# Ordering the products that use a part of the TensorE array, with four key tiles and two weight staging tiles, in a decoder layer with sparse attention

## The chip, the core and the metric

The kernel runs on one core of a Trainium2 chip. TensorE (PE) multiplies: it holds a stationary operand in its array of 128 x 128 cells, streams a moving operand through it and writes PSUM. VectorE (DVE), ScalarE (ACT) and GpSimd (POOL) compute; SyncE (SP) issues most loads, POOL issues the gathers by index. The metric is the device time of one execution in microseconds (us), lower is better. Products of 128 x 32 cells use one of four column groups of the array, products of 128 x 64 one of two, and products over 64 rows one of two row groups; products on different groups can be in the array at the same time.

## What is computed

One inference step of a decoder layer for a prompt of 512 tokens and for 8 samples of 4 new tokens each, whose 4096 past keys and values lie in pages of a cache. Model width 1024, hidden width of the feed-forward 2816. Cut to what matters here:

```python
x = x + 0.5 * swiglu(rmsnorm(x), ffn1)
h = rmsnorm(x)
gb, gc, hc, q, k, v, qi, ki, wi = split(h @ w_in)     # 3 x 512, 512, 128, 128, 512, 64, 8 columns
y_conv = gb * short_conv(gc * hc)                     # depthwise, width 3
I[t, s] = sum_h wi[t, h] * relu(qi[t, h] . ki[s])     # indexer, 8 heads of 64
idx = top_k(I masked causally)                        # 128 of the prompt's, 256 of a sample's 4100 keys
attn = softmax(q . k[idx] / 8) @ v[idx]               # 8 query heads of 64 on 2 key heads
x = x + concat(y_conv, attn) @ w_out
x = x + 0.5 * swiglu(rmsnorm(x), ffn2)
```

All is fp32. The selected keys aren't gathered one by one: all logits are made, and those not selected get a bias of -1e30.

## The kernel before, in words

The activations lie transposed on the chip, 544 tokens (32 of the samples, 512 of the prompt) in columns. The weights of the feed-forward layers, of w_in and of w_out are streamed (`stream`, L155): a staging tile wst of 128 x 1024 fp32 (tag "wst", WB of them) is loaded by SP, ACT rounds it to a high part whi, DVE or POOL subtracts that to get a low part wlo, and PE then makes three products (high by high, high by low, low by high) in fp32r at one pass each. whi and wlo have three places ("slots"). wst is free again when wlo is made, except in `nat` for the 32 sample tokens (i = 0, L522), which multiplies by the fp32 tile itself, a quarter of the products in each column group. `load_half` (L588) loads the columns of one group of w_in in runs of k-tiles: two tiles for most groups, three (KS) for the second half of the indexer's columns, which comes first.

Between the feed-forward layers lies the mixer (L1307). Its parts are Python generators, each a row of steps, and `plan` (L1255) emits the steps in order of a start and a spacing for each part (PLAN for the first half, PLAN2 for the second). The framework then orders the instructions of each engine by priority and by when their operands and buffers are expected to be there; LAG shifts the priority of a part, and parts in PINNED keep the program's order on PE. What an engine issues is fixed when the program is built. The parts: A, B indexer columns; Q, K queries, keys and values; S the samples' indexer scores; V the exact search of each sample query's 256th best score (DVE, three searches of two bits a round), which ends with `self.bias` (L870); I, D the prompt's scores and selection (DVE); L the raw logits of the first four samples; e, c the gated convolution in four chunks, with three tiles of w_in columns each (e, the chunks 0 and 1, uses slot 2 only); then s the attention of the samples, P that of the prompt, w the first half of w_out.

The products that the change touches:

- S, `sample_scores` (L709): for each of 8 steps (a half of the pages and a pair of samples) two gathers of index keys by POOL, each transposed by PE in `key_transpose` (L699, eight transposes to PSUM "KTp", copied by ACT to one of KTB tiles "KT"); `scores` (L743) then multiplies them for the pair, 64 columns of the array each, two halves of 512 keys (ssc); `gathered` (L754) sums heads for four pairs, 32 columns each (SC).
- L and s, `qk` (L1023): logits of one quarter of the pages for four samples. For each sample a gather of keys and a key_transpose; two products of 32 columns and 512 keys each (lg) follow, LGD = 2 samples behind. Each sample writes its own 32 partitions of one PSUM tile with tag "w".
- s, `pv` (L1094): the values of a quarter: four gathers, eight transposes of the weights (PT), 32 products of 32 columns (O), four samples for each of eight key tiles.
- `sample_attend` (L1121): after the softmax of samples 0 to 3, four times pv of these and qk of samples 4 to 7, then the softmax and four pv of these. Keys and values share KV = 4 gather tiles.
- P, `prompt_softmax` (L1156): for a block of 128 queries four logits products over 64 rows of the array (plg), each into its own PSUM tile with tag "f", and read by DVE.

PSUM has tags w (two tiles of two banks; used by KTp, lg, ssc, PT and the feed-forward's G, U, Y), f (two of one bank), s and t (one each). `mm` (L129) issues a product; `keep_in_program_order` pins it.

Of the kernel before, what the change touches and what calls it, by code (L numbers as in the profile page):

```python
# [15 lines left out]
ALU = mybir.AluOpType  # L16
# [30 lines left out]
WB = 3  # L47
# [9 lines left out]
LGD = 2  # L57
KTB = 3
# [59 lines left out]
class Trunk:  # L118
# [14 lines left out]
    def tp(self, *args):  # L133
        ins = self.nc.tensor.transpose(*args)  # L134
        return self.tc.keep_in_program_order(ins) if self.pin else ins

# [18 lines left out]
    def stream(self, srcs, n, m, kind="", slot=None):  # L155
        """fp32 weights [128, n, m] from DRAM, as the two float32r parts, in the given or the next place of three."""
# [25 lines left out]
    def wmm(self, unit, parts, act, cuts=HALVES, which=(0, 1)):  # L182
        """unit[:, i, :] = W^T act over all k-tiles, for the ith cut of the tokens; W stationary."""
# [10 lines left out]
    def fmm(self, name, parts, act, n):  # L194
        """two PSUM banks, one per half of the tokens: W^T act over n k-tiles."""
# [35 lines left out]
    def rms(self, ssq):  # L231
        """sums of squares [128 tokens, 5 tiles] -> rn, 1 / root mean square."""
# [19 lines left out]
    def spread(self):  # L252
        """R [128, T]: the row of rn on every partition."""
# [9 lines left out]
    def ffn(self, wg, wu, wd, done, late=False):  # L263
# [3 lines left out]
        def hidden(f, G, U):  # L267
            """G, U: one PSUM tile of equal halves, or (columns, PSUM) pairs."""
# [95 lines left out]
    def begin_units(self):  # L364
        """loads and transposes the activations; the first gate and up units, by halves of the tokens as these come in."""
        nc, tc, i = self.nc, self.tc, self.i
        with tc.tile_pool(name="init", bufs=1) as ip, tc.high_priority(offset=FIRST):
# [13 lines left out]
            def weights(w, n):  # L381
                """w's first 128 columns in n runs of k-tiles: for each a function that loads it, fp32 and the two parts."""
# [57 lines left out]
            def mms(unit, w, hf, order="01234567" * 2):  # L440
                """the high parts of the weights at a k-tile's first mention, the low ones at its second."""
# [80 lines left out]
    def nat(self, i, wparts, m):  # L522
        """steps; PSUM [tokens of tile i, m]. The few samples take a column group of the array each for a quarter of the
        fp32 products, and the four sums are added at the end."""
# [29 lines left out]
    def rope(self, v, i, n, nh, kind):  # L554
        """partial rotary on v [n tokens, nh, 64] of token tile i."""
# [32 lines left out]
    def load_half(self, pieces, m, ks=(4, 4), slots=(0, 1)):  # L588
        """w_in columns in runs of ks k-tiles, [128, k, m] each; pieces: (offset in tile, first column, width)."""
# [8 lines left out]
    def later(self, f, depth):  # L598
        """keep f for later; run what lies deeper than depth."""
        if f:  # L600
            self.held.append(f)
        while len(self.held) > depth:
            self.held.pop(0)()

    def idx_group(self, g, i, parts, depth=0):
        """steps; four indexer query heads of token tile i, and for g = 1 the indexer keys and head weights."""
# [45 lines left out]
    def qkv_group(self, g, i, parts, depth=0):  # L652
        """steps; four query heads of token tile i (g: 0, 1), or its keys and values (g: 2)."""
# [45 lines left out]
    def key_transpose(self, kn, name):  # L699
        """eight 128 x 128 transposes of gathered keys, PSUM -> SBUF."""  # L700
# [8 lines left out]
    def sample_scores(self, mp):  # L709
        """indexer scores of the sample queries over all pages: [128 = (bp, jh, b2, rr, t), (jl, p)]."""  # L710
# [20 lines left out]
        def headsum(out, S, bp, jh):  # L731
            self.mm(out, wm[:, bp, jh, :], S, start=True, stop=True)
# [10 lines left out]
        def scores(n):  # L743
            bp = n % 4
            w = self.wunit("ssc")
            for hf in range(2):
                for b2 in range(2):
                    self.mm(w[64 * b2:64 * b2 + 64, hf, :], self.qbi[:, 2 * bp + b2].rearrange("p r t h -> p (r t h)"),
                            kts[n, b2][:, hf * 512:(hf + 1) * 512], start=True, stop=True)
# [4 lines left out]
        def gathered(jh, c):  # L754
            u = self.tunit("SC")
            for bp in range(4):
                headsum(u[32 * bp:32 * bp + 32, :], SS[bp][:, c * 512:(c + 1) * 512], bp, jh)
# [43 lines left out]
    def sample_select(self, mp):  # L801
        """exact top K_S of the 4100 scores of each query (ties: lowest position first) -> bias 0 / -BIG."""
# [16 lines left out]
        def search(src, bits, base0):  # L819
            """[128, 1]: the largest x of base0 to base0 + 2**bits - 1 with K_S elements of the query at or above x,  # L820
            two bits a round: three candidates, counted on the vector engine (two) and the scalar engine."""
# [82 lines left out]
    def prompt_scores(self, pool):  # L904
        """indexer scores of prompt blocks 1..3, causally filled; block 0 keeps every admissible key."""
# [27 lines left out]
    def prompt_select(self, pool, scores):  # L933
        """the top K_P of the scores of each query (ties: lowest position first) -> 0 / -BIG."""
# [13 lines left out]
    def conv(self, cs, pool, early=False):  # L948
        """steps; the gated convolution of the channel chunks cs."""
# [73 lines left out]
    def qk(self, st, q, more):  # L1023
        """PSUM: raw logits of quarter q of the pages, samples 4 st to 4 st + 3; rows (b, g, c, t)."""
        nc = self.nc
        kts, w = [], None

        def logits(b4):
            for rr in range(2):
                self.mm(w[32 * b4:32 * b4 + 32, rr, :], self.qbd[:, 4 * st + b4].rearrange("p g c t -> p (g c t)"),  # L1030
                        kts[b4][:, rr], start=True, stop=not more)

        for b4 in range(4):
# [3 lines left out]
            if b4 >= LGD:  # L1037
                w = w or self.wunit("lg")
                logits(b4 - LGD)
        for b4 in range(4 - LGD, 4):  # L1040
            yield
            w = w or self.wunit("lg")
            logits(b4)
# [195 lines left out]
    def until(self, mark, steps):  # L1239
        """advance steps until mark is reached."""  # L1240
        while mark not in self.done:
            next(steps)
# [273 lines left out]
```

## Time and profile before

| | |
|---|---|
| three runs | 1279.54, 1279.09, 1273.50 us, median 1279.09 |
| profiled execution, span from first to last instruction | 1270.2 us; its device time is not in the profile |
| PE busy | 1230.0 us, 97% |
| DVE, ACT, POOL busy | 640.4, 456.4, 209.3 us |
| stages | feed-forward 1 to about 411 us, mixer to about 860 us, feed-forward 2 |
| mean granted TensorE clock | 0.995 of full |

The span runs from the first to the last instruction of the core; the device time of a run has some more around it. Busy times are unions: an fp32 product shows as two matmul records, a record's duration runs to its modelled end, and records that overlap count once. A group of products that run one behind the other and one that run together can so have the same mean duration; the union and the starts tell them apart.

### The profile page before, as it was taken

What the parts mean: (1) busy time and instruction counts of PE and PEld (TensorE: products, weight loads), DVE (VectorE), ACT (ScalarE), POOL (GpSimd) and SP (SyncE); (2) the same over time, 40 slices, a digit from 0 to 9 for tenths busy, and PEclk for the clock granted to TensorE, in tenths of its full rate; (3) what the DMA queues carried; (4) which work ended last, traced back from release to release, by engine and by line L of the source; (5) the groups of instructions that cost most, each with busy time, mean ns of one, the idle gap of its engine ahead of it and who ended that gap; (6) DMA issues with size and microseconds to landing.
All of it is one profiled execution on the core that took longest, in us unless ns stands there. A gap on an engine that the chain in (4) does not pass through costs nothing.

```text
span 1270.2 us, 22873 instructions
## 1 busy us (share of the span) xinstructions
PE 1230.0 (97%) x9629; PEld 1112.8 (88%) x9629; DVE 640.4 (50%) x1230; ACT 456.4 (36%) x696; POOL 209.3 (16%) x319
## 2 busy tenths in 40 slices
PE   9999999999999999899989989999999999999998
PEld 8999999999999747776667545789999999999998
DVE  5444334433446216999999753265443344433442
ACT  6332122212224464456525556244222122222222
POOL 3200000000000646665413231310000000000000
PEclk9999999999999999999999999999999999999999
DMA  7422332332222553245224443543223323322322
GB/s 231 133 85 84 93 90 84 92 92 84 86 73 69 179 178 106 68 138 169 68 61 140 161 151 124 167 141 113 87 84 93 91 84 87 96 85 84 91 75 74
DMA packets 184363, 136.10 MB, mean 107 GB/s; under 512 B 5706, under 2 KB 172434, under 8 KB 184260
## 3 DMA queue, kind: packets, MB, share of 16 engines
q1 hardware_dynamic: 171700, 91.62, 24.7%
q0 software_dynamic: 11904, 42.26, 10.3%
q8 instruction: 76, 1.25, 0.4%
q10 hardware_dynamic: 656, 0.76, 0.2%
q14 instruction: 27, 0.22, 0.1%
HBM read 131.66 MB, written 2.96 MB: 106 GB/s over the span
## 4 chain that ended last, share of the span: by engine, by line
PE 83%; DVE 10%; DMA 2%; issue 2%; ACT 1%; POOL 1%; DVEq 0%; ACTq 0%; POOLq 0%
PE Y L191 20%; PE U L191 20%; PE G L191 19%; PE Yo L130 4%; DVE flip L829 3%; PE KTp L134 2%; PE lg L130 2%; PE nat L130 2%; DMA ckn<-in_cache_k,ik 2%; PE O L130 2%; PE ssc L130 1%; PE plg L130 1%; PE pO L130 1%; DVE pw L928 1%; PE gc L130 1%
## 5 line engine op out<-in xcount | busy, mean ns | idle before, releaser
L166 ACT ACTIVATE whi<-wst 128x1024 fp32r<-128x1024 f32 (+3 forms) x173 | 172.7, 999 | 582.6 <-PE Y L191 181.2
L171 DVE TENSOR_TENSOR wlo<-wst,whi 128x1024 fp32r<-128x1024 f32 (+3 forms) x156 | 180.7, 1158 | 26.8 <-ACT whi L166 23.1
L191 PE MATMUL Y<-hh,wlo 128*128 128x272 f32 (+2 forms) x704 | 147.6, 288 | 0.0
L191 PE MATMUL Y<-hh,whi 128*128 128x272 f32 (+2 forms) x704 | 147.4, 289 | 0.0
L191 PE MATMUL Y<-hl,whi 128*128 128x272 f32 (+2 forms) x704 | 147.1, 288 | 0.0
L191 PE MATMUL U<-xh,whi 128*128 128x272 f32 x688 | 142.0, 287 | 1.5 <-DVE t L274 1.5
L191 PE MATMUL U<-xh,wlo 128*128 128x272 f32 x688 | 141.6, 288 | 0.0
L191 PE MATMUL U<-xl,whi 128*128 128x272 f32 x688 | 141.3, 287 | 0.0
L191 PE MATMUL G<-xh,whi 128*128 128x272 f32 x656 | 135.6, 287 | 0.0
L191 PE MATMUL G<-xl,whi 128*128 128x272 f32 x656 | 135.0, 287 | 0.0
L191 PE MATMUL G<-xh,wlo 128*128 128x272 f32 x656 | 134.9, 288 | 0.0
L276 DVE TENSOR_TENSOR u<-U,R 128x544 f32<-128x544 f32 x43 | 31.2, 725 | 160.2 <-PE U L191 160.2
L191 PEld LDWEIGHTS Y<-hl,whi 128*128 128x128 f32 x704 | 111.4, 188 | 0.0
L191 PEld LDWEIGHTS Y<-hh,whi 128*128 128x128 f32 x704 | 111.1, 188 | 0.0
L191 PEld LDWEIGHTS Y<-hh,wlo 128*128 128x128 f32 x704 | 110.7, 189 | 0.0
L330 DVE SCALAR_TENSOR_TENSOR x<-Y,x 128x544 f32<-128x544 f32 x46 | 33.3, 725 | 152.2 <-PE Y L191 152.2
L191 PEld LDWEIGHTS U<-xh,whi 128*128 128x128 f32 x688 | 107.1, 188 | 1.6 <-ACT whi L166 1.6
L191 PEld LDWEIGHTS U<-xl,whi 128*128 128x128 f32 x688 | 107.5, 188 | 0.0
L191 PEld LDWEIGHTS U<-xh,wlo 128*128 128x128 f32 x688 | 107.1, 189 | 0.0
L169 POOL TENSOR_TENSOR wlo<-wst,whi 128x1024 fp32r<-128x1024 f32 (+2 forms) x17 | 34.4, 2025 | 423.4 <-ACT whi L166 422.8
L191 PEld LDWEIGHTS G<-xl,whi 128*128 128x128 f32 x656 | 102.6, 188 | 0.0
L191 PEld LDWEIGHTS G<-xh,whi 128*128 128x128 f32 x656 | 102.2, 188 | 0.0
(330 smaller groups left out, 2235.0 us busy)
## 6 DMA issues: line engine op xcount, KB each, us to landing
wst<-in_ffn_w_up SPq DMA_DIRECT2D x44, 512.0 KB, 3.7
wst<-in_ffn_w_gate SPq DMA_DIRECT2D x43, 512.0 KB
wst<-in_ffn_w_down SPq DMA_DIRECT2D x32, 512.0 KB, 4.1
wst<-in_w_in SPq DMA_DIRECT2D x16, 512.0 KB, 4.0
wst<-in_ffn_w_down SPq DMA_DIRECT2D x16, 384.0 KB, 3.5
xn<-in_x_prompt SPq DMA_DIRECT2D x4, 512.0 KB
wst<-in_w_in SPq DMA_DIRECT2D x8, 256.0 KB, 8.9
wst<-in_w_out SPq DMA_DIRECT2D x8, 256.0 KB, 2.6
```

The source lines that it names most:

```text
L130: ins = self.nc.tensor.matmul(*args, **kw)
L134: ins = self.nc.tensor.transpose(*args)
L166: nc.scalar.activation(hi, st, AF.Copy)
L169: nc.gpsimd.tensor_tensor(lo, st, hi.bitcast(F32), op=ALU.subtract)
L171: nc.vector.tensor_sub(lo, st, hi.bitcast(F32))
L191: self.nc.tensor.matmul(unit[:, i, :c1 - c0], a[:, k, :], b[:, k, c0:c1], start=k == 0 and j == 0, stop=k == n - 1 and j == 2)
L276: nc.vector.tensor_mul(dst.rearrange("p (a b) -> p a b", a=2), src[:, :, :HT], self.R.rearrange("p (a b) -> p a b", a=2))
L330: nc.vector.scalar_tensor_tensor(xc, Y[:, :, :HT], 0.5, xc, op0=ALU.mult, op1=ALU.add)
L829: V.tensor_scalar(junk, src, cand[:, k:k + 1], None, op0=ALU.is_ge, op1=ALU.add, accum_out=cnt[:, k:k + 1])
L928: nc.vector.scalar_tensor_tensor(W, t, wcol, W, op0=ALU.mult, op1=ALU.add)
```

## The change

`in_a_row` is new: it issues the first of the given products, then all others right behind it on PE, at a high priority (RUN). The first is the one whose operand comes last. ssc, SC, lg, O and plg are issued through it, with the products on different parts of the array next to each other. lg waits for all four key tiles of a quarter, then issues first halves of four samples and second halves of four samples; so KTB is 4 instead of 3, and WB is 2 instead of 3 in return for the space. plg takes one tile of tag w for two products in place of two tiles of tag f. Docstrings are dropped.

```diff
-WB = 3
+WB = 2
-LGD = 2
-KTB = 3
+KTB = 4
+RUN = 5000
+    def in_a_row(self, last, *others):
+        with self.tc.high_priority(offset=RUN):
+            with self.tc.issue_after(last().ins):
+                for f in others:
+                    f()
...
         def headsum(out, S, bp, jh):
-            self.mm(out, wm[:, bp, jh, :], S, start=True, stop=True)
+            return self.mm(out, wm[:, bp, jh, :], S, start=True, stop=True)
...
             w = self.wunit("ssc")
-            for hf in range(2):
-                for b2 in range(2):
-                    self.mm(w[64 * b2:64 * b2 + 64, hf, :], self.qbi[:, 2 * bp + b2].rearrange("p r t h -> p (r t h)"),
-                            kts[n, b2][:, hf * 512:(hf + 1) * 512], start=True, stop=True)
+            def part(hf, b2):
+                return lambda: self.mm(w[64 * b2:64 * b2 + 64, hf, :], self.qbi[:, 2 * bp + b2].rearrange("p r t h -> p (r t h)"),
+                                       kts[n, b2][:, hf * 512:(hf + 1) * 512], start=True, stop=True)
+            self.in_a_row(*[part(hf, b2) for hf in range(2) for b2 in (1, 0)])
...
             u = self.tunit("SC")
-            for bp in range(4):
-                headsum(u[32 * bp:32 * bp + 32, :], SS[bp][:, c * 512:(c + 1) * 512], bp, jh)
+            self.in_a_row(*[lambda bp=bp: headsum(u[32 * bp:32 * bp + 32, :], SS[bp][:, c * 512:(c + 1) * 512], bp, jh)
+                            for bp in (3, 0, 1, 2)])
...
     def qk(self, st, q, more):
-        kts, w = [], None
-        def logits(b4):
-            for rr in range(2):
-                self.mm(w[32 * b4:32 * b4 + 32, rr, :], self.qbd[:, 4 * st + b4].rearrange("p g c t -> p (g c t)"),
-                        kts[b4][:, rr], start=True, stop=not more)
+        kts = []
         for b4 in range(4):
             kn = self.gather(self.kvp, self.i["cache_k"], 1024, self.ik[:, q, 4 * st + b4:4 * st + b4 + 1], "ckn", "kv", KV)
             kts.append(self.key_transpose(kn, "KT").rearrange("p (a r b) -> p r a b", r=2, b=128))
             yield
-            if b4 >= LGD:
-                w = w or self.wunit("lg")
-                logits(b4 - LGD)
-        for b4 in range(4 - LGD, 4):
-            yield
-            w = w or self.wunit("lg")
-            logits(b4)
+        yield
+        w = self.wunit("lg")
+        def logits(rr, b4):
+            return lambda: self.mm(w[32 * b4:32 * b4 + 32, rr, :], self.qbd[:, 4 * st + b4].rearrange("p g c t -> p (g c t)"),
+                                   kts[b4][:, rr], start=True, stop=not more)
+        self.in_a_row(*[logits(rr, b4) for rr in range(2) for b4 in (3, 0, 1, 2)])
+        yield
         return w
...
-        for c in range(8):
+        def part(c, b4):
             r = 2 * (c % 4) + c // 4
-            for b4 in range(4):
-                self.mm(O[32 * b4:32 * b4 + 32, :128], pt[:, c, 32 * b4:32 * b4 + 32],
-                                 vs[b4][:, r * 128:(r + 1) * 128], start=False, stop=q == 3 and c == 7)
+            return lambda: self.mm(O[32 * b4:32 * b4 + 32, :128], pt[:, c, 32 * b4:32 * b4 + 32],
+                                   vs[b4][:, r * 128:(r + 1) * 128], start=False, stop=q == 3 and c == 7)
+        self.in_a_row(*[part(c, b4) for c in range(8) for b4 in (3, 0, 1, 2)])
...
-        for s in (0, 2, 1, 3):
-            g, c = divmod(s, 2)
-            gs = slice(64 * g, 64 * g + 64)
-            w = self.funit("plg")
-            self.mm(w[:, :N], self.qT[gs, 2 * ch + c, q0:q0 + 128], self.kT[gs, NS:NS + N], start=True, stop=True)
-            nc.vector.tensor_tensor_reduce(P[:, s, :N], w[:, :N], self.pw[j], 0.125, -3.0e38, op0=ALU.add, op1=ALU.max,
-                                           accum_out=mx[:, s:s + 1])
+        for c in range(2):
+            w = self.wunit("plg")
+            def logits(g):
+                gs = slice(64 * g, 64 * g + 64)
+                return lambda: self.mm(w[:, g, :N], self.qT[gs, 2 * ch + c, q0:q0 + 128], self.kT[gs, NS:NS + N], start=True, stop=True)
+            self.in_a_row(logits(0), logits(1))
+            for g in range(2):
+                s = 2 * g + c
+                nc.vector.tensor_tensor_reduce(P[:, s, :N], w[:, g, :N], self.pw[j], 0.125, -3.0e38, op0=ALU.add, op1=ALU.max,
+                                               accum_out=mx[:, s:s + 1])
```

## Rows read from the trace of the kernel before

**Rows 1.** The page: busy us (share of the span) xinstructions.

```profile
PE 1230.0 (97%) x9629; PEld 1112.8 (88%) x9629; DVE 640.4 (50%) x1230; ACT 456.4 (36%) x696; POOL 209.3 (16%) x319
```

**Rows 2.** Stretches of the mixer: length, busy us of PE, PEld, DVE, ACT, POOL, clock, DMA.

```profile
400.00:485.00 85.00, 83.93 (x543) 54.72 (x542) 21.88 (x45) 43.27 (x71) 38.57 (x77) 1.00 0.52 158
485.00:680.00 195.00, 174.36 (x1214) 139.73 (x1212) 185.07 (x493) 100.78 (x168) 97.84 (x158) 0.97 0.31 91
680.00:785.00 105.00, 98.11 (x787) 59.71 (x779) 64.92 (x205) 55.64 (x117) 33.03 (x36) 1.00 0.51 169
785.00:840.00 55.00, 51.72 (x529) 39.84 (x527) 15.62 (x39) 20.92 (x41) 16.98 (x16) 1.00 0.48 154
```

**Rows 3.** Timeline of DVE, the bias: start, us, instruction.

```profile
651.34 0.49 DVE L870 TENSOR_SCALAR bias<-low,base 128x1056 bf16<-128x1056 uint16 x1
```

**Rows 4.** Groups of PE's instructions: xcount, busy us, mean ns, idle before.

```profile
L130 PE MATMUL lg<-KT,qbd 128*32 128x512 f32 x128 | 40.9, 598 | 0.0
L130 PE MATMUL plg<-kTs,qTs 64*128 64x128 f32 (+3 forms) x64 | 21.4, 482 | 1.0 <-ACT pPTs L1192 0.7 <-DVE pmx L1168 0.2
L130 PE MATMUL O<-cvn,PTs 128*32 128x128 f32 x512 | 19.0, 274 | 0.8 <-DMA cvn<-in_cache_v,ik 0.8
L130 PE MATMUL ssc<-kt,qbi 128*64 128x512 f32 x64 | 18.0, 607 | 0.0
...
L130 PE MATMUL SC<-Srel,wm 128*32 128x512 f32 x32 | 10.5, 605 | 0.1
```

**Rows 5.** Timeline of PE, single bursts: start, us, instruction, xcount.

```profile
538.56 1.93 PE L130 MATMUL lg<-KT,qbd 128*32 128x512 f32 x12
...
546.18 1.90 PE L130 MATMUL lg<-KT,qbd 128*32 128x512 f32 x4
...
446.49 1.04 PE L130 MATMUL SC<-Srel,wm 128*32 128x512 f32 x2
...
463.67 1.07 PE L130 MATMUL SC<-Srel,wm 128*32 128x512 f32 x8
```

**Rows 6.** The chain of waits, 700 to 740 us: start, us, what.

```profile
705.83 2.01 PE O L130 x64
...
709.34 5.05 DMA ckn<-in_cache_k,ik
...
720.65 1.83 PE lg L130 x4
722.49 1.02 PE KTp L134 x8
...
731.60 1.88 PE O L130 x64
```

**Rows 7.** A stretch, plg alone: length, PE, PEld and DVE busy, clock, DMA.

```profile
680.00:785.00 105.00, 17.61 (x53) 6.51 (x53) 12.25 (x27) 1.00 0.51 169
```

**Rows 8.** Timeline of POOL, the fourth gather of values; in brackets the idle before it.

```profile
723.78 0.94 POOL L695 DMA_INDIRECT cvn<-in_cache_v,ik  x1 [4.79 <-PE KTp L134]
```

**Rows 9.** Timeline of SP's issues of weight tiles and ACT's conversions.

```profile
102.95 0.37 SPq L163 DMA_DIRECT2D wst<-in_ffn_w_down  x1
...
106.01 1.06 ACT L166 ACTIVATE whi<-wst 128x1024 fp32r<-128x1024 f32 x1 [3.53 <-PE G L191]
111.98 1.06 ACT L166 ACTIVATE whi<-wst 128x1024 fp32r<-128x1024 f32 x1 [4.35 <-issue]
...
13.44 0.37 SPq L163 DMA_DIRECT2D wst<-in_ffn_w_up  x1
```

**Rows 10.** The view of tile wst: from issue to landing, over the whole span.

```profile
DMA to landing us min/median/max: 2.5/3.8/8.9
```

**Rows 11.** Timeline of SP and ACT: a weight tile's issue and the next tiles' conversion.

```profile
437.74 0.94 SPq L163 DMA_DIRECT2D wst<-in_w_in  x2
...
505.10 1.06 ACT L166 ACTIVATE whi<-wst 128x1024 fp32r<-128x1024 f32 x1 [1.32 <-PE nat L130]
```

**Rows 12.** A stretch of PE: length, busy us (xcount), granted clock, DMA.

```profile
522.00:526.00 4.00, 1.85 (x8) 0.75 0.00 0
```

## The prediction, made before the changed kernel ran

> **What bounds the kernel now.** I read four views in this order. First the page's busy shares [rows 1]: TensorE (PE) is busy for 97% of the span, VectorE (DVE) for half. So work taken from PE counts, unless another engine ends last in the stage it is taken from. Second, the stretches of the middle [rows 2], where all edited products lie; the reader should compare PE with DVE in each. From 400 to 485 us PE is busy 83.9 of 85 us: PE bounds it. From 485 to 680 us DVE is busy 185.1 of 195 us: DVE bounds it, and it ends with the bias of the search at 651 us, on which the samples' masked softmax waits [rows 3]. From 680 to 785 us PE has 98.1 of 105 us, from 785 to 840 us 51.7 of 55, but there a second chain, the gathers of the cache, runs beside it. The two feed-forward layers on both sides are pure PE and are not edited except for their staging tiles. Third, the groups of products [rows 4], for how much PE time there is to win. Fourth, the timeline of single bursts [rows 5], for what a burst costs that does run side by side.
>
> **What side by side is worth.** An fp32 product shows as two matmul records. The key: 12 records of the cache logits (lg), three samples whose turn came together, took 1.93 us, and 4 records, one sample alone, took 1.90 us [rows 5]. So one sample more costs nothing. The same is seen at SC: 8 records (all four column groups) in 1.07 us, 2 records in 1.04 us. The kernel before already does this where its order happens to put products next to each other; the change makes it always so. By group:
> - lg: 8 quarters of four samples, 40.9 us now [rows 4]. After: one burst a quarter, priced as the burst of three, 8 x 1.95 = 15.6 us. Saved 25.3.
> - ssc: 18.0 us now; two groups of columns, so 8 records in four places, as long as a burst of lg: 8 x 1.94 = 15.5. Saved 2.5.
> - SC: 10.5 us now, after 4 x 1.07 = 4.3. Saved 6.2.
> - O (values): 19.0 us now; 64 records, all of one quarter, stand in the chain with 2.01 and 1.88 us [rows 6], so after 8 x 1.95 = 15.6. Saved 3.4.
> - plg (prompt logits, two row groups): 21.4 us for 64 records; pairs would take half of it and a few tails, I take 12. Saved 9.4.
> Together 46.8 us of PE. The rest of this part is how much of it reaches the end.
>
> The trace prices the fourth group at nothing (1.07 against 1.04). The Trainium skill, TensorE: Matmul & The Clock Gate, Part 3 (Packing small matmuls), gives 3.07 times for four tiles, not 4; by it a quarter of lg would take 4 x 1.90 / 3.07 = 2.48 us (an estimate from that page), and the sum below would be some 2 us smaller. I stay with the rows.
>
> **400 to 485 us.** ssc saves 2.5; of SC, the 16 records that run two at a time (8 x 1.04 = 8.3 us) become two bursts (2.1): 6.2 saved, all of it in this stage. Bounds: 8.7 if PE alone bounds, 3 if the gathers of index keys end last in part of it (DMA share 0.52). I take 6, nearer to PE's 83.9 of 85. **485 to 680 us.** Half of the lg quarters lie here, some 20 us that become 7.8; but the cover is DVE, which has 10 us idle in 195. I take 0; bounds a gain of 5 (the prompt's selection can start earlier) and a loss of 4. **680 to 785 us.** The other half of lg is here, 20.4 us that become 7.8: 12.6 go; plg has 17.6 us [rows 7], 8 go: 20.6 of 98.1. The chain of the samples is what decides: from one burst of values to the next, 705.83 to 731.60, is 25.8 us [rows 6]. In it the fourth key transpose stands on PE behind two lg bursts of 1.83 us (the second is shown [rows 6]), and so the fourth value gather leaves POOL 4.8 us late, waiting for that transpose [rows 8]; the next values need it. After the change all logits come behind the last transpose, so the two bursts leave that place: 4 us shorter a quarter, 4 quarters, 16 us. Bounds: 4 (only 1 us a quarter, when the gathers' landing of 5.05 us [rows 6] takes over) and 20.6. What is late next is that landing. **785 to 840 us.** Half of O's 3.4 and a little of plg go here, but each quarter waits for four gathers; I take 1, bounds 0 and 5.
>
> **Two weight tiles for three.** In the feed-forward layers a tile lasts for 48 products, and the next is converted 6 us later, at 106.01 and 111.98. The buffer converted before these is loaded again from 102.95 us [rows 9] and lands 3.8 us later (median, 8.9 at most [rows 10]), at 106.8; with two buffers it is wanted at 111.98: 5 us in hand, cost 0. If that cover went (a landing of 8.9), it would be just reached. At the start the third tile now waits for the first tile's parts, as the fourth did, till 13.44 [rows 9], and PE lacks its products as a filling for about one landing: 0 to 3.8 us, I take 1.5. At the mixer's begin three tiles (the pieces of the index columns) are held until the samples' products have read their fp32 form; with two, the third is issued only when the first has been read, and PE waits for a landing (3.8, up to 8.9) with a few transposes to fill: 0 to 5, I take 3. From 437.74 to 505.10 us one tile lay loaded and unconverted [rows 11], a place that vanishes: the convolution's second load then waits behind the queries' two. DVE's bound covers it; I take 0, bounds 0 and 10. The fourth key tile (KTB) and the plg pairs in the wider PSUM buffers (tag w, two of them) add no instruction; a pair holds a buffer until DVE has read both halves, and key transposes, lg and PT queue behind it for that tag. I cost that at nothing because 680 to 785 has DVE free for 40 of 105 us; without this cover it is part of the 4 us bound. The new ordering adds no wait on another engine: the first product of a row waits for the latest operand, and what is queued behind it on PE is held that long, at most a key copy of some 1 us, 8 times, inside the bounds above.
>
> **The clock.** From 522 to 526 us, after an idle stretch, PE was granted 0.75 in the mean and did 8 products in 1.85 us [rows 12], 0.23 each instead of 0.12. More idle between 485 and 680 may bring one or two such drops (2.4 to 1.2 GHz), under DVE's cover; 1 us for one outside it.
>
> **Sum.** -6 + 0 - 16 - 1 + 1.5 + 3 + 0 + 1 = -17.5 us on the profiled span of 1270.2 us, so 1252.7. No row tells what lies around that span; the median of the runs, 1279.1, is 8.9 above it, the lowest, 1273.5, is 3.3. Taking off the same from the median gives 1261.6, **1262 us**. The change's own bounds: all good ends (-8.7 - 5 - 20.6 - 5) give 1240; all bad ends (-3 + 4 - 4 + 3.8 + 5 + 10 + 2) give 1297.
>
> **Rivals.**
> - *The gathers take over* (0.18). The quarter of 25.8 us stays near it, since the landings of 5.05 us and four gathers of half a megabyte at 169 GB/s [rows 2] decide. For: they stand in the chain [rows 6]. Against: POOL's last gather waited for PE, not for a landing [rows 8]. Then -6 - 4 - 1 + 5.5: about 1274.
> - *The weight tiles starve* (0.13), the slower side. Place: 437 to 520 us, the early convolution, six tiles of 48 products, 6 us each by the pace above, 36 us of PE that fill DVE's stage. The queries' two tiles hold both buffers, the convolution's load follows only when the second queries are converted, after 505.10 [rows 11], and its products slide behind 680, where PE bounds. Decides once more slides than the 23 us won; if all but 2 slide, 1279 - 23 + 34 + 5 = 1295, with 28 sliding 1289. Against: DVE bounds the stage up to 651 us [rows 3], so products that come 10 or 20 us later still find PE's idle time.
> - *The products don't run together* (0.09): the change doesn't do what it says. A product's second record uses the same columns as its first; if it held back the next product's first, four products would take 5 places instead of 2, SC and lg would save almost nothing (8 x 2 x 5 x 0.47 = 37.6 against 40.9 us), and the time would be 1279 - 3 + 4.5, about 1280. Against: the 12 records in 1.93 us are four places of three. The Trainium skill, same page and part, says matmuls start and end in strict order; that would make this rival, and the trace disagrees as far as one burst tells.
>
> **How the numbers follow.** The forecast has 0.60. A measurement of this kernel tells about 0.5% (6.4 us) from no change: faster is below 1272.7, slower above 1285.5. The forecast's own range, 1248 to 1272, is faster; of the gather rival a third is; the third rival is the same. Faster 0.60 + 0.05 = 0.65, same 0.12 + 0.08 = 0.20, slower 0.15 with the starving rival and a little of the third. The range runs from the good bounds, less their least likely corner, 1246, to above the gather rival and the third, 1281.
>
> **What would show it.** Right: lg at 32 places, busy near 16 us; SC in bursts of 8; the values' bursts 21 to 22 us apart; DVE still at 185 of 195 in its stage, starting 3 us earlier. Wrong: an unchanged distance of those bursts with DMA in the chain (gathers); convolution products after 720 us, or a weight load waiting on a query product (starving); records of lg 0.43 us apart (no running together).

## The result, and the profile of the kernel after

The kernel after takes 1307.9 us, the kernel before 1278.4 in the same comparison: a ratio of 1.0237 (95% interval 1.0205 to 1.0269). It is slower by 30 us; 1262 had been predicted. The profiled execution of after has a span of 1305.7 us, 35.5 more than that of before. Spans on record lie 1.8 us below the times of their runs, so the profiled execution of before was a short one, about 1272 us; the medians are 29.6 us apart.

**The products do run together.** The groups of products on PE, whole span, as [rows 4] for before (columns: line, engine, operation, output<-inputs, shapes, count | busy us, mean ns | idle us before them and what ended it):

```profile
L130 PE MATMUL O<-cvn,PTs 128*32 128x128 f32 x512 | 20.7, 329 | 28.4 <-DMA cvn<-in_cache_v,ik 27.4 <-ACT PTs L1107 1.0
L130 PE MATMUL ssc<-kt,qbi 128*64 128x512 f32 x64 | 15.5, 605 | 1.4 <-issue 0.9 <-ACT kt L714 0.5
L130 PE MATMUL lg<-KT,qbd 128*32 128x512 f32 x128 | 15.4, 598 | 2.3 <-ACT KT L714 1.7 <-DVE pmx L1177 0.7
L130 PE MATMUL plg<-kTs,qTs 64*128 64x128 f32 (+3 forms) x64 | 12.8, 486 | 1.6 <-ACT KT L714 1.4 <-DVE pmx L1177 0.2
L130 PE MATMUL SC<-Srel,wm 128*32 128x512 f32 x32 | 5.1, 718 | 1.7 <-ACT Srel L760 1.7
```

lg fell from 40.9 to 15.4 us, plg from 21.4 to 12.8, SC from 10.5 to 5.1, each as forecast within a us. And PE is no longer what bounds: 97% busy before [rows 1], 93% now, with 27.4 us in which the value products wait for their gathers, 0.8 before [rows 4]. The page's row of busy times:

```profile
PE 1209.1 (93%) x9629; PEld 1121.4 (86%) x9629; DVE 639.3 (49%) x1230; ACT 455.6 (35%) x696; POOL 206.5 (16%) x319
```

**Where the time went.** The stretches of after, as [rows 2], with one more (length, busy us of PE, PEld, DVE, ACT, POOL, granted clock, DMA share, GB/s):

```profile
400.00:485.00 85.00, 74.41 (x499) 52.74 (x499) 21.32 (x41) 41.84 (x68) 37.32 (x75) 0.94 0.43 136
...
785.00:840.00 55.00, 36.89 (x373) 29.47 (x371) 9.79 (x24) 18.11 (x27) 16.11 (x17) 0.85 0.57 177
840.00:875.00 35.00, 13.25 (x201) 10.82 (x202) 2.72 (x6) 4.71 (x7) 7.49 (x8) 0.65 0.36 120
```

The last stretch of before:

```profile
840.00:875.00 35.00, 34.96 (x275) 34.20 (x274) 24.47 (x41) 17.55 (x27) 1.46 (x2) 1.00 0.37 106
```

PE idles in three places: some 11 us in 400 to 485, where before it had 83.9 of 85; 10 us between the first two bursts of values below; and 40 us in 785 to 875, where before it had 3. The bursts of values date the rest. Timeline of PE in after (start, us, instruction, count [idle before <-what ended it]):

```profile
691.67 1.96 PE L130 MATMUL O<-cvn,PTs 128*32 128x128 f32 x64
745.42 1.95 PE L130 MATMUL O<-cvn,PTs 128*32 128x128 f32 x64 [0.99 <-ACT PTs L1107]
773.51 1.96 PE L130 MATMUL O<-cvn,PTs 128*32 128x128 f32 x64
798.76 1.96 PE L130 MATMUL O<-cvn,PTs 128*32 128x128 f32 x64
827.88 1.96 PE L130 MATMUL O<-cvn,PTs 128*32 128x128 f32 x64
839.97 3.64 PE L130 MATMUL O<-cvn,PTs 128*32 128x128 f32 x64 [7.76 <-DMA cvn<-in_cache_v,ik]
853.23 3.64 PE L130 MATMUL O<-cvn,PTs 128*32 128x128 f32 x64 [9.62 <-DMA cvn<-in_cache_v,ik]
866.92 3.64 PE L130 MATMUL O<-cvn,PTs 128*32 128x128 f32 x64 [10.05 <-DMA cvn<-in_cache_v,ik]
```

The same in before (the second and third burst are in [rows 6]):

```profile
680.60 1.96 PE L130 MATMUL O<-cvn,PTs 128*32 128x128 f32 x64
...
756.38 1.95 PE L130 MATMUL O<-cvn,PTs 128*32 128x128 f32 x64
792.18 1.96 PE L130 MATMUL O<-cvn,PTs 128*32 128x128 f32 x64
```

The first burst is 11.1 us late. From it to the second, the "first quarter" of the expectations below, are 53.7 us instead of 25.2: 28.5 lost at one place. The later distances (28.1, 25.3, 29.1 against 25.8, 24.9, 35.8) give only some 4 us back, and the last three rounds of values another 1.3 (42.7 us from the fifth burst's start to the last one's end, 44.0 in before). So the last values end 34.4 us later (870.6 for 836.1), and what follows them takes 435 us in after and 434 in before: the chain of the samples sets the end.

In that quarter the fourth key transpose is the late one. Timeline of PE in after:

```profile
704.93 1.09 PE L134 MATMUL KTp<-main,ckn 128*128 128x128 f32 x8 [0.57 <-DVE pmx L1177]
707.14 0.92 PE L130 MATMUL plg<-kTs,qTs 64*128 64x128 f32 x8 [1.11 <-ACT KT L714]
...
715.60 0.49 PE L134 MATMUL KTp<-main,ckn 128*128 128x128 f32 x3
716.02 0.92 PE L130 MATMUL plg<-kTs,qTs 64*128 64x384 f32 x4
716.87 0.77 PE L134 MATMUL KTp<-main,ckn 128*128 128x128 f32 x5
```

The third transpose is at 704.9, the fourth at 715.6, with pairs of the prompt's logits between; the last product of plg starts at 747.8, in before at 787.4. Of its 64 records 60 start in the first quarter, in before 8. The prompt ran first, the samples waited. POOL shows the same in its gathers (timeline of POOL in after):

```profile
706.30 0.94 POOL L703 DMA_INDIRECT cvn<-in_cache_v,ik  x1 [2.73 <-PE KTp L134]
717.91 1.02 POOL L703 DMA_INDIRECT cvn<-in_cache_v,ik  x1 [10.67 <-PE KTp L134]
747.62 0.94 POOL L703 DMA_INDIRECT ckn<-in_cache_k,ik  x1 [28.70 <-PE O L130]
```

The wait for the fourth transpose, 4.8 us in [rows 8], which I had expected to shorten, is 10.7; the next quarter's gathers then wait 28.7 us for the values. In these 53.7 us PE is busy for 43.3, with the prompt's products and the convolution's. w_out's first half, the last of its other work, runs from 751.9 to 805 us, so in the last rounds only the gathers are left.

What a pair waits for, and who waits for a pair, can be read in some places (timelines of DVE and PE in after). DVE reads the pairs of 707.14 only at 712.36, when the transposes of an earlier unit have read the tile of the prompt's weights (P), and the pair of 730.62 at 738.76, right behind the selection (pw). The samples' logits and the transpose of their weights end PE's idle time with such a read (pmx, L1177):

```profile
712.36 0.29 DVE L1177 CUSTOM_DVE_ANT_0 P<-plg,main 128x128 f32<-128x128 f32 x1 [1.01 <-PE pPT L134]
...
738.76 0.69 DVE L1177 CUSTOM_DVE_ANT_0 P<-plg,pw 128x512 f32<-128x512 f32 x1 [0.17 <-DVE pw L953]
...
728.22 1.93 PE L130 MATMUL lg<-KT,qbd 128*32 128x512 f32 x16 [0.65 <-DVE pmx L1177]
...
742.28 1.09 PE L134 MATMUL PT<-main,L 128*128 128x128 f32 x8 [0.23 <-DVE pmx L1177]
```

Of the 11 us before that burst 8.6 are there when the search starts (495.8 for 487.2). The products of the third piece of the index columns waited for its load (groups of PE, 400 to 485 us of after; in before the same 32 records had no idle time).

```profile
L130 PE MATMUL nat<-wst,xs 128*32 128x328 f32 (+1 forms) x32 | 5.0, 458 | 7.1 <-DMA wst<-in_w_in 7.1
```

Stretches of after around that wait:

```profile
422.00:428.00 6.00, 0.04 (x1) 0.00 (x0) 1.86 (x2) 0.00 (x0) 2.80 (x5) 0.68 0.96 312
428.00:436.00 8.00, 6.36 (x27) 4.31 (x27) 1.35 (x3) 1.92 (x5) 2.27 (x10) 0.60 0.38 113
```

PE stands still from 422 to 428, and over the next 8 us its granted clock is 0.60 in the mean, nearer to 1.2 than to 2.4 GHz. The DMA engines are at a share of 0.96 in the wait: the index keys' gathers are in flight with that load.

### The profile page after: what moved, and what is told of

Its sections match the earlier page's. It is cut to its first block, busy times and chain, and to the rows that moved or that the text cites. A ratio compares the mean times of both kernels' runs of the same rounds, so it can differ in the third digit from the quotient of the medians.

```text
span 1305.7 us, 22878 instructions
## 1 busy us (share of the span) xinstructions
PE 1209.1 (93%) x9629; PEld 1121.4 (86%) x9629; DVE 639.3 (49%) x1230; ACT 455.6 (35%) x696; POOL 206.5 (16%) x319
## 4 chain that ended last, share of the span: by engine, by line
PE 74%; DVE 14%; DMA 4%; ACT 3%; issue 2%; POOL 1%; SPq 0%; ACTq 0%; DVEq 0%; POOLq 0%
PE Y L199 20%; PE U L199 20%; PE G L199 19%; PE Yo L130 4%; DVE flip L838 4%; PE KTp L134 2%; PE nat L130 2%; PE O L130 2%; DMA cvn<-in_cache_v,ik 1%; PE gc L130 1%; DVE pw L951 1%; DMA wst<-in_w_in 1%; PE gb L130 1%; DVE m L950 1%; DMA ckn<-in_cache_k,ik 1%
## 5 line engine op out<-in xcount | busy, mean ns | idle before, releaser
L199 PEld LDWEIGHTS G<-xh,wlo 128*128 128x128 f32 x656 | 102.2, 189 | 0.0
```

The lines of the kernel that those rows point to most:

```text
L199: self.nc.tensor.matmul(unit[:, i, :c1 - c0], a[:, k, :], b[:, k, c0:c1], start=k == 0 and j == 0, stop=k == n - 1 and j == 2)
```

## The experiments

The theories: 1, the prompt's part (plg) does it; 2, two staging tiles do; 3, logits of four at a time do. All ratios are to the kernel before, in the same comparison.

**One part undone, three ways, and one part alone.**

e1, in `prompt_softmax` of after, the loop of before again:

```diff
-        for c in range(2):
-            w = self.wunit("plg")
...
+        for s in (0, 2, 1, 3):
+            g, c = divmod(s, 2)
...
+            w = self.funit("plg")
```

e2 and e3, on after:

```diff
-            self.in_a_row(logits(0), logits(1))
+            with self.tc.issue_after(logits(0)().ins):
+                logits(1)()
```

```diff
-            w = self.wunit("plg")
+            w = [self.funit("plg") for _ in range(2)]
```

e4, on the kernel before:

```diff
-WB = 3
+WB = 2
```

> The kernel after, with the prompt's logits (plg) made as before: four single products, each in its own tile of tag f, no raised priority. Theory 1 (the prompt's pairs delay the samples' chain): the first quarter, 53.7 us from the first burst of values to the second in the kernel after, falls back to 22 to 28 us, and the time to about 1308 - 28 = 1280 us (1272 to 1288). Theory 2 (two weight staging tiles are the main cost): the quarter may change, but the time stays above 1295. Theory 3 (logits of four at a time hold the samples' chain): the first quarter stays above 45 us and the time within 6 us of 1308.

Measured: 1279.2 us, ratio 1.0015 (0.9996 to 1.0034). The first quarter is 21.4 us and the next two 22.0 and 21.8 (timeline of PE):

```profile
691.96 1.96 PE L130 MATMUL O<-cvn,PTs 128*32 128x128 f32 x64
713.41 1.95 PE L130 MATMUL O<-cvn,PTs 128*32 128x128 f32 x64 [0.20 <-DMA cvn<-in_cache_v,ik]
735.41 1.95 PE L130 MATMUL O<-cvn,PTs 128*32 128x128 f32 x64 [0.24 <-ACT PTs L1107]
757.21 1.95 PE L130 MATMUL O<-cvn,PTs 128*32 128x128 f32 x64 [0.24 <-ACT PTs L1107]
```

Theory 1 holds for these 28 us; 3 falls, since the logits of four are still in.

> The kernel after, with the prompt's logits still in pairs and in tag w, the second behind the first, but without the raised priority. Theory 1a (the priority is what puts the prompt ahead): 1275 to 1288 us, plg ends again near 785 us. Theory 1b (holding a tile of tag w until VectorE has read it is what delays the key transposes): 1300 to 1312 us, first quarter above 45 us. Theories 2 and 3: 1300 to 1312 us.

Measured: 1309.1 us, 1.0268 (1.0228 to 1.0308). It isn't the priority.

> The kernel after, with the prompt's logits in pairs at the raised priority, but each in its own tile of tag f as in the kernel before, so that no tile of tag w waits for VectorE. Theory 1a (priority): 1300 to 1312 us. Theory 1b (tag w): 1275 to 1288 us, first quarter back at 22 to 28 us. Theories 2 and 3: 1300 to 1312 us.

Measured: 1275.6 us, 0.9992 (0.9971 to 1.0013); first quarter 23.5 us. It is tag w. (With own tiles of tag f, 44 of the 64 records no longer stand in pairs: plg costs 21.3 us of PE again, and that hardly matters.)

> The kernel before, with two weight staging tiles in place of three and nothing else. Theory 1: only the start and the mixer's begin pay, 1.4 + 7.2 us by the traces, so 1278 + 5 to 10 = 1283 to 1289 us. Theory 2 (staging tiles are the main cost): 1295 us or more, convolution products behind 720 us.

Measured: 1292.9 us, 1.0120 (1.0093 to 1.0146), above theory 1's 1283 to 1289 and below theory 2's 1295. The search starts 13.5 us late (500.7 for 487.2), and the same products wait:

```profile
L130 PE MATMUL nat<-wst,xs 128*32 128x328 f32 (+1 forms) x20 | 3.8, 498 | 5.5 <-DMA wst<-in_w_in 5.5
```

The last convolution product is at 731 us (710.9 before); the whole stage is late, so that mark of theory 2 doesn't tell where it comes from. e10 tells more.

**Parts alone, and the order.** e5 is the kernel before with `in_a_row` and the `prompt_softmax` of after, so of the diff only the hunk of plg. e6, on e3, in `load_half`:

```diff
+            if len(parts) == 2:
+                st = self.kvp.tile([128, 1024], F32, name="wi2", tag="kv", bufs=KV)[:, :n * m]
```

e7 is after with `qk` and `prompt_softmax` as before, and

```diff
-WB = 2
-KTB = 4
+WB = 3
+LGD = 2
+KTB = 3
```

e8, on after, in LAG:

```diff
-'P': 500
+'P': 4000
```

> The kernel before with one part of the change alone: the prompt's logits in pairs in tag w (three staging tiles, three key tiles, all other products as before). Theory 1b (the pairs take tag w from the samples' chain): the first quarter goes from 25 us to over 40 us and the time to 1295 to 1310 us. Rival (the pairs hurt only together with four key tiles and logits of four at a time): 1272 to 1282 us, quarters near 25 us.

Measured: 1327.5 us, 1.0383 (1.0355 to 1.0410); bursts at 685.96 and 748.94, a first quarter of 63.0 us. The part alone costs 48 us, more than the theory's range, so it needs neither four key tiles nor logits of four.

> The kernel of e3 (pairs of the prompt's logits in tag f), and the third piece of the index columns staged in a free tile of the gathers instead of a third weight staging tile. Theory (two staging tiles cost some 12 us at the mixer's begin, and PE bounds from there on): no wait of 5 to 7 us on that piece at 422 to 429 us, the search starts at 482 to 486 instead of 493 us, time 1263 to 1269 us, ratio to before 0.987 to 0.993. Rival (the rest of the two-tile cost lies in the convolution's staging, and VectorE's stage takes the gain back): 1272 to 1277 us, ratio 0.995 to 1.0.

Measured: 1273.9 us, 0.9968 (0.9949 to 0.9986). The wait is gone and the search starts at 486.0 instead of 493.0, as the theory says, but the time falls short of it and is the rival's. The gain is lost later, though not where the rival puts it: the bias still comes 7 us earlier (651.8 for 659.0), but the fourth to the fifth burst are 39.6 us (36.9 in e3) and PE has 41.3 us of 55 from 785 on. The lead over e3 is 6.9 us at the fourth burst, 4.2 at the fifth, 1.9 at the sixth and 0.9 at the last. Why those distances grew was not settled.

> The kernel before with only the index scores (ssc), their head sums (SC) and the value products (O) issued in a row; three staging tiles, three key tiles, logits of samples and prompt as before. Theory (my step for 400 to 485 us, 6 us): the search starts at 480 to 483 instead of 487 us and the time is 1270 to 1275 us, ratio 0.993 to 0.998. Rival (the gathers of index keys end last there, or the gain is lost behind VectorE's stage): start of the search above 485 us, ratio 0.998 to 1.002.

Measured: 1269.6 us, 0.9928 (0.9905 to 0.9950): 0.7% less than before, the interval clear of 1. The search starts at 481.0, 6.2 us earlier.

> The kernel after, with the priority of the prompt's attention (P) put back by 3500 and nothing else; its pairs stay in tag w. Theory 1b in the form that the order among tag w's users decides, with VectorE in the middle of the prompt's selection: the samples go first, the first quarter falls below 35 us and the time to 1278 to 1292 us. Rival (each pair delays the samples for as long as VectorE needs, wherever it stands): the 28 us only spread over the other quarters, 1300 us or more.

Measured: 1312.6 us, 1.0277 (1.0252 to 1.0302). plg starts from 701.5 to 753.8, about as early as in after (698.7 to 747.8), and the first quarter is 55.5 us: a lower priority doesn't put the prompt back, so the order is set elsewhere. The pairs themselves keep the raise of `in_a_row` here, so e8 lowers only the rest of the prompt's chain; e2 had taken the raise away.

**What sets the order.** e9, on after, in the plan of the second half (PLAN2):

```diff
-'P': (44, 7.25)
+'P': (44, 20)
```

e10 is e4 with the edit of e6. e11, on e7, gives samples 4 to 7 the `qk` of after (as `qk4`) and its fourth key tile from the attention's pool:

```diff
-            w = yield from self.qk(1, q, True)
+            w = yield from self.qk4(1, q, ap)
...
+            kts.append(self.key_transpose(kn, "KT", ap if b4 == 3 else None).rearrange("p (a r b) -> p r a b", r=2, b=128))
```

> The kernel after, with the steps of the prompt's attention emitted 20 apart instead of 7.25 in the plan of the second half, so that they are spread over three of the samples' four quarters instead of the first one and a half; its pairs stay in tag w. Theory 1c (the tiles of tag w go round in the order in which the plan emits their users, and that order, not a priority and not VectorE, makes the first quarter wait for the prompt): plg ends after 770 us, the first quarter falls to 28 to 36 us, the others rise by a few us, time 1282 to 1296 us. Rival (a pair holds its tile until VectorE is out of the prompt's selection, whatever the order): the time stays within 6 us of 1308.

Measured: 1309.9 us, 1.0242 (1.0217 to 1.0268). The first quarter fell to 29.5 us, as theory 1c says, but the second took 54.2 (timeline of PE; the burst between starts at 719.56):

```profile
771.70 1.09 PE L134 MATMUL pPT<-main,P 128*128 128x128 f32 x8
773.78 1.95 PE L130 MATMUL O<-cvn,PTs 128*32 128x128 f32 x64 [0.98 <-ACT PTs L1107]
```

The wait moved with the plan and did not shrink: the time is the rival's and not the 1282 to 1296 of theory 1c, so later runs ask what the pairs wait for.

> The kernel of e4 (the kernel before with two weight staging tiles), and the third piece of the index columns staged in a free tile of the gathers. Theory (what two tiles cost is the wait for that piece and the low clock behind it): the search starts at 487 to 491 us instead of 500.7, time 1277 to 1284 us, ratio to before 1.0 to 1.004. Rival (the convolution's staging pays a large part too): 1286 us or more.

Measured: 1283.7 us, 1.0038 (1.0021 to 1.0055). Of the 1.2% of e4, 0.8% (10.5 us) is the third piece; the search starts at 489.7. What is left, 5 us, was not taken apart. In its profile the last convolution product starts at 722.8 us (710.9 in before) though the search starts only 2.6 us late, and the first quarter is 31.9 us (25.2), so the convolution's staging has a part in it.

> The kernel of e7 (before, with ssc, SC and O in a row; three staging tiles) and the logits of samples 4 to 7 made four at a time as in the kernel after, the fourth key tile taken from the pool of the samples' attention; the prompt's logits as before. Theory (my step for 680 to 785 us): the quarters fall from 27.2, 26.0, 26.3 in e7 to 21 to 23 us, the last values end some 11 us earlier than in e7, time 1256 to 1264 us, ratio to before 0.982 to 0.989. Rival (the gathers of the last four value bursts, about 14 us each, and the lack of other work for PE there take the gain back): 1266 to 1271 us.

Measured: 1256.5 us, 0.9816 (0.9791 to 0.9841): 1.8% less than before, and the fastest kernel of all. The quarters are 23.3, 20.9 and 22.6 us (timeline of PE):

```profile
677.60 1.95 PE L131 MATMUL O<-cvn,PTs 128*32 128x128 f32 x64
700.89 1.96 PE L131 MATMUL O<-cvn,PTs 128*32 128x128 f32 x64
721.83 1.96 PE L131 MATMUL O<-cvn,PTs 128*32 128x128 f32 x64
744.41 1.96 PE L131 MATMUL O<-cvn,PTs 128*32 128x128 f32 x64
```

PE stays full behind them, where after had 36.9 and 13.3 us (stretches of e11):

```profile
785.00:840.00 55.00, 50.31 (x518) 44.62 (x517) 23.83 (x44) 19.96 (x33) 12.65 (x12) 1.00 0.49 151
840.00:875.00 35.00, 35.00 (x281) 34.65 (x280) 20.15 (x31) 15.31 (x23) 2.15 (x1) 1.00 0.40 116
```

**What the pairs wait for.**

All four on after: e12 in `prompt_softmax`, e13 in `prompt_select`, e14 in PLAN2, e15 in `prompt_softmax`.

```diff
-                nc.vector.tensor_tensor_reduce(P[:, s, :N], w[:, g, :N], self.pw[j], 0.125, -3.0e38, op0=ALU.add, op1=ALU.max,
+                with self.tc.high_priority(offset=RUN):
+                    nc.vector.tensor_tensor_reduce(P[:, s, :N], w[:, g, :N], self.kT[:, :N], 0.125, -3.0e38, op0=ALU.add, op1=ALU.max,
```

```diff
+                if r < 1:
                     m8 = pool.tile([128, 8], F32, name="m8", tag="m8", bufs=2)
```

```diff
-'P': (44, 7.25)
+'P': (480, 7.25)
```

```diff
-        P = ap.tile([128, 4, 256 if j < 2 else 512], F32, name="P", tag=f"P{j // 2}", bufs=1)
+        P = ap.tile([128, 4, 256 if j < 2 else 512], F32, name="P", tag=f"P{j // 2}", bufs=2)
```

> The kernel after, where VectorE's read of each prompt pair (plg) adds the prompt's keys, ready since the first half, in place of the selection's mask, and goes at a raised priority; the selection itself is still made, its mask is left out of the prompt's softmax. So a pair's tile of tag w waits neither for the selection of its block nor behind it on VectorE. Theory 1d (the pairs of the selected blocks hold tag w until VectorE has finished the selection, and the samples' next key transposes, logits and weights stand behind them): the first quarter falls from 53.7 to 22 to 30 us, the time to 1276 to 1288 us. Rival (two tiles of tag w are too few for prompt and samples together, whatever the pairs wait for): quarters above 35 us and 1300 us or more.

Measured: 1309.3 us, 1.0243 (1.0216 to 1.0270); first quarter 53.1 us. The wait for the selection's mask alone isn't it.

> The kernel after, with one of sixteen rounds of the prompt's selection left (the other rounds are left out, so the prompt attends with too small a selection); pairs in tag w. Theory 1e (VectorE, busy with the selection, reads the pairs late, and that is what holds tag w): the first quarter falls from 53.7 to under 32 us. Rival 1f (the prompt's chain itself, eight units of pair, VectorE, ScalarE, VectorE and PE, is pulled ahead of the samples by the order in which the plan emits the users of tag w): the first quarter stays above 42 us. The time also holds what VectorE saves before 680 us, so the quarter decides.

Measured: 1303.4 us, 1.0212 (1.0184 to 1.0239); the quarter is 60.2 us (677.9 to 738.1). VectorE's occupation alone isn't it.

> The kernel after, with the prompt's attention emitted behind the samples' four quarters of logits (start 480 instead of 44 in the plan of the second half); pairs still in tag w. Theory 1f (the plan's order of tag w's users): all three quarter distances 21 to 25 us, plg starts after 765 us, and the prompt's chain of some 50 us (698 to 748 in the kernel after) runs beside the last four value bursts, so 1275 to 1295 us. Rival (two tiles of tag w are too few for both, in any order): quarters above 30 us or a time of 1300 us or more.

Measured: 1291.7 us, 1.0118 (1.0080 to 1.0156). plg runs from 776.2 to 843.3, and the quarters are 23.0, 22.1 and 23.8 us with the pairs still in tag w (timeline of PE):

```profile
689.72 1.96 PE L130 MATMUL O<-cvn,PTs 128*32 128x128 f32 x64
712.74 1.96 PE L130 MATMUL O<-cvn,PTs 128*32 128x128 f32 x64
734.79 1.95 PE L130 MATMUL O<-cvn,PTs 128*32 128x128 f32 x64
758.64 3.64 PE L130 MATMUL O<-cvn,PTs 128*32 128x128 f32 x64 [3.95 <-DMA cvn<-in_cache_v,ik]
```

The plan's order of the users of tag w decides: theory 1f. The time is not won back: the values end at 838.0 us, but the prompt's chain now runs last (its last logits start at 843.3), and the kernel keeps the two staging tiles, which alone cost 15 us in e4.

> The kernel after, with two tiles in place of one for the prompt's weights of each size (P0, P1), so that a pair need not wait until the values of the unit two before have read theirs. Theory 1g (this wait inside the prompt's chain is what makes the pairs hold tag w long): first quarter under 42 us, time under 1298 us. Theory 1f: first quarter within 5 us of 53.7, 1303 to 1314 us.

Measured: 1308.8 us, 1.0247 (1.0220 to 1.0274); first quarter 56.1 us. That wait inside the prompt's chain alone isn't it. e12, e13 and e15 each took away one wait of the pairs; whether several of them hold the pairs in turn, so that removing one changes nothing, was not tested.

**The order in the traces.** From PLAN2 and the steps of the parts s and P follows the order in which the plan hands out the tiles of tag w. For after it is, from the first quarter's PT on (each plg is a pair in one tile):

```text
PT KTp plg plg KTp plg plg KTp plg plg KTp plg plg plg plg lg plg plg plg plg PT plg plg KTp KTp KTp KTp lg ...
```

PE's first writes into these tiles, read from its timeline, come in exactly this order, for all 40 tiles up to the fourth quarter's logits, in after and in e2, e8, e12, e13 and e15, whatever the priority and the load of VectorE. In e9 they come in the order of its own plan, again for all 40. With the pairs in tag f they don't follow the plan: in before the first quarter begins PT, plg, KTp, plg, KTp, KTp, and only 8 of plg's 64 records start in it.

## Why the prediction was wrong

**Side by side: right.** 15.4 us of lg were measured for 15.6 forecast, 15.5 for 15.5 of ssc, 12.8 for 12 of plg, 5.1 for 4.3 of SC. O has 20.7 for 15.6, because its last three bursts take 3.64 us instead of 1.95, at a granted clock of 0.50 (1.2 GHz), which is a consequence. The rival "don't run together" is out: one quarter of lg, in 691 to 746 us of after, is

```profile
L130 PE MATMUL lg<-KT,qbd 128*32 128x512 f32 x16 | 1.9, 598 | 0.7 <-DVE pmx L1177 0.7
```

16 records of four samples in the time that 4 records of one took [rows 5]. The estimate of 2.48 us from the 3.07 times of the Trainium skill (TensorE: Matmul & The Clock Gate, Part 3, Packing small matmuls) does not hold here; that page's figure is for four tiles of rows, lg uses four groups of columns, and the measurement decides.

**400 to 485 us, -6: right.** Alone (e7) the three groups issued in a row (ssc, SC, O) bring the search 6.2 us forward, and the whole time falls by 0.72% (9 us).

**680 to 785 us, -16: the mechanism right, the size a little off.** Where the prompt doesn't share the tag, the distances are 21 to 23 us (e1, e11), 21 to 22 forecast. But only three distances shrink: the fourth, 35.8 us before and 36.0 in e1, holds the softmax of the second four samples. From e7 to e11 the time falls from 0.9928 to 0.9816 of before, 14 us.

**The step that failed: "I cost that at nothing because 680 to 785 has DVE free for 40 of 105 us".** It asked only whether an engine is busy enough to hold the tiles. Taken alone, neither DVE's load (e13) nor the order of its reads (e12) nor the priority (e2, e8) is it: the quarter does not shorten. What the step left out is the order of the tiles. Two chains that had their own buffers came to share two. With tag f the prompt's logits could stay behind while the samples went ahead; before, plg started from 677.8 to 787.4 us. In tag w the tiles go round in the order of the plan, and the plan emits the pairs of seven of the prompt's eight units between the first quarter's PT (14.75) and the second's (132.75). So a key transpose emitted behind a pair gets its tile only when the pair's is read, and the second burst of values waits until the pairs of seven units are read: 28.5 us in the profile. The measured time lies above even the prediction's sum of all bad ends, 1297 us. Shown are the tag (e1, e3, e5), the plan's order (e14, and the order of the tiles in the traces) and that a spread plan only moves the wait (e9). Open is what sets the pace of a unit, some 7 us (the pairs of the eight units start over 49 us).

The 35.5 us between the spans are the chain of the samples: 11.1 us before the first burst and 28.5 behind it, less 5.3 later. The 40 us of idle PE behind 785 go with it, but don't add to it: the last three rounds take their gathers' time in both kernels (42.7 and 44.0 us), with PE idle in after and full in before. Before, w_out's first half and the values ended together (834 and 836 us); after, at 805 and 871.

**The term that was mis-sized: the mixer's begin, 3 (0 to 5).** It measured 10.5 us (e4 less e10). The place and the mechanism were right, "the third is issued only when the first has been read". But the landing was taken from the median of 3.8 us, and this load goes out when the gathers of the index keys have the DMA engines at a share of 0.96; PE waited 7.1 us, and behind the wait the granted clock was 0.60. The few transposes that were to fill it did not come: PE had 0.04 of 6 us. The rival "weight tiles starve" named 1289 to 1295 us for the early convolution. That e4 measured 1292.9 is chance: 10.5 of its 15 us are the third piece, and at most the 5 us of e10 are left for the convolution.

**What the parts don't add up to.** Two tiles (+15), the rows (-9) and the logits of four (-14) make -8; the kernel with just these parts (e1) measured +2, e3 -1. In e1 some 7 us of the 10 can be seen: the last values end at 834.5 us, 1.6 earlier than in before, but 83 of the 192 records of w_out's first half still start behind them, in before none, and from the values' end to the end of the span are 441.8 us instead of 434.1. What is missing in e3 stays open, as does the place behind the fourth burst where e6 lost its gain.

## What to carry to other kernels

A product moved into another buffer tag is not free because the engines are: ask whose tiles go round in that tag, and in which order they are handed out, since a chain that could lag is then in front of the one that decides. Where an idle engine is offered as the cover of a wait, ask also which chain ends last: here PE had other work for most of the wait, and the time was lost all the same, because the samples' chain stood still. And a wait for a load is priced by the landing at that moment, with what else is on the DMA engines, not by the median.

## What was not expected of the hardware

Four fp32 products of 32 columns each cost as much as one, 16 records in 1.9 us for 4 in 1.90. After the 7.1 us without a product, the granted clock over the next 8 us was 0.60, and the bursts of values that follow idle stretches of 8 to 10 us took 3.64 us instead of 1.95, at 0.50: here an idle PE paid a second time when it started again.
